# Splitting the first loads of a fused add and LayerNorm into 8-row transfers

## The chip, the cores and the metric

One core of a Trainium2 chip. The metric is device microseconds of the whole program on that core. A change of 2% would be 4.8 us.

## The reference

```python
z = x + residual                       # x, residual: (16, 1024, 512) float32
mean = np.mean(z, axis=-1, keepdims=True)
var = np.var(z, axis=-1, keepdims=True)
z_norm = (z - mean) / np.sqrt(var + eps)
return (gamma * z_norm + beta).astype(np.float32)
```

The 16,384 vectors of 512 numbers are laid over 128 partitions, so each partition has 128 of them. The kernel calls one such step of all partitions a "row": 128 x 512 x 4 bytes, 262,144 bytes. There are 128 rows of x, 128 of the residual and 128 of the output to move: 384 row moves.

## The kernel before

All transfers are issued from the sync engine's queue, in the order of a plan. `x48+16` is a load of rows 48 to 63 of x, `r` is the residual, `o` an output store.

```python
PLAN = """
x0+8 r0+8 x8+8 r8+8 x16+16 r16+16 x32+16 r32+16 x48+16
o0+16 r48+16 x64+12 o16+20 r64+16 x76+24 r80+16 o36+28
r96+16 x100+8 x108+20 r112+4 r116+12
o64+16 o80+28 o108+12 o120+4 o124+4
"""
```

Buffers hold 64 rows of x (reused for the result) and 32 rows of the residual (reused for the sum). Three kinds of issue therefore wait, and as the sync engine issues in order, everything behind a waiting issue waits too:

```python
if kind == "x":                                  # its z rows must have been stored
    while gone < len(stores) and stores[gone][0] < lo + n - Z_ROWS:
        nc.sync.wait_ge(so[gone], 16)            # the store has landed
        gone += 1
    ...
elif kind == "r":                                # its r rows must have been used
    if lo + n > R_ROWS:
        last = (lo + n - R_ROWS) // TURN - 1
        nc.sync.wait_ge(s_rstd[last % Z_TURNS], last // Z_TURNS + 1)
    ...
else:                                            # the result must be there
    nc.sync.wait_ge(s_out, lo + n)
```

The compute goes in turns of 4 rows: POOL adds, ACT makes the mean and the sum of squares with two passes per row and then the root, DVE normalises with two passes per row.

```python
nc.gpsimd.tensor_tensor(out=z, in0=part(zbuf, Z_ROWS, lo, n), in1=z, op=ALU.add)   # z: the r rows
...
act.activation(out=junk_m[k][:, :], in_=part(rbuf, R_ROWS, r, 1), func=ACT.Identity,
               scale=-inv_d, accum_out=column(nm, r))
...
act.activation(out=junk_s[k][:, :], in_=part(rbuf, R_ROWS, r, 1), func=ACT.Square,
               bias=column(nm, r), accum_out=column(ssq, r))
...
dve.scalar_tensor_tensor(out=part(zbuf, Z_ROWS, r, 1), in0=part(rbuf, R_ROWS, r, 1),
               scalar=column(nm, r), in1=gamma_p[:, :], op0=ALU.add, op1=ALU.mult)
# then reciprocal -> s_rstd (frees the r rows), then the second pass -> s_out
```

## Time and profile before

| | before |
|---|---|
| time, median of 3 runs | 237.92 us (237.81 to 237.95) |
| span of the profiled run | 236.5 us |
| bytes moved | 67.11 MB read, 33.55 MB written |
| busy: DVE, ACT, POOL | 75%, 78%, 61% |
| transfers on the sync queue | 27 |

The span is from the first to the last instruction; the time is about 1.4 us longer. The prediction below shows the slices, the queue, the chain and the waits. The groups of instructions give the durations that it works with: count, busy time, mean of one in ns, then the engine's idle time ahead of the group and what ended most of it.

```profile
L178 POOL TENSOR_TENSOR rbuf<-zbuf,rbuf 128x2048 f32<-128x2048 f32 x32 | 143.9, 4526 | 66.6 <-DMA rbuf<-in_residual_dram 62.1
L201 ACT ACTIVATE junk_m<-rbuf 128x512 f32<-128x512 f32 x128 | 74.3, 580 | 32.7 <-POOL rbuf L178 32.5
```

The large idle times on the right are what invites the change: POOL waits 62 us for loads, ACT 32 us for POOL. One of ACT's waits is the hole that the prediction speaks of, before its fifth turn:

```profile
45.98 0.60 ACT L201 ACTIVATE junk_m<-rbuf 128x512 f32<-128x512 f32 x1 [6.15 <-POOL rbuf L178]
```

### The profile page before, as it was taken

To read this page: it belongs to the slowest core of one execution; us is meant where nothing else is said; L and a number is where in the kernel's file an instruction comes from. 1 tells how busy PE (TensorE), PEld (TensorE's weight loads), DVE (VectorE), ACT (ScalarE), POOL (GpSimd) and SP (SyncE) were. 2 spreads that over 40 slices of the span, in tenths; PEclk is the share of its full clock that TensorE was granted. 3 is DMA by queue.
4 is the path that set the end of the run, shared out by engine and by line. 5 is a ranking of instruction groups with operands and counts; after the bars stand their busy time and mean duration, and the time that the engine had idled before them with its cause. 6 is when DMAs were issued, how large, how long until landed. Compare 5 with 4: busy or idle time off the path is not lost.

```text
span 236.5 us, 992 instructions
## 1 busy us (share of the span) xinstructions
PE 3.7 (2%) x4; PEld 1.2 (0%) x4; DVE 177.2 (75%) x290; ACT 183.8 (78%) x545; POOL 144.1 (61%) x36
## 2 busy tenths in 40 slices
PE   0600000000000000000000000000000000000000
PEld 0100000000000000000000000000000000000000
DVE  0001999629999999589990999889993999999930
ACT  2019997299999996899909999899939999999400
POOL 0098920999799306993079846993199498960000
DMA  8999999999999999998999999989999999998997
GB/s 316 438 435 435 421 438 443 443 443 443 427 371 438 443 421 423 470 436 384 443 449 474 391 427 499 398 389 432 416 454 429 417 442 435 489 436 388 411 410 327
DMA packets 3893, 100.68 MB, mean 426 GB/s; under 512 B 434, under 2 KB 434, under 8 KB 436
## 3 DMA queue, kind: packets, MB, share of 16 engines
q1 hardware_dynamic: 3888, 100.67, 99.4%
q14 instruction: 1, 0.01, 0.0%
q10 hardware_dynamic: 4, 0.00, 0.0%
HBM read 67.11 MB, written 33.55 MB: 426 GB/s over the span
## 4 chain that ended last, share of the span: by engine, by line
ACT 48%; DMA 35%; POOL 6%; DVE 4%; issue 1%; SPq 1%; ACTq 0%; DVEq 0%; POOLq 0%
DMA rbuf<-in_residual_dram 35%; ACT junk_s L211 25%; ACT junk_m L201 21%; POOL rbuf L178 6%; DVE zbuf L239 3%; ACT std L220 2%; DVE zbuf L253 1%; SPq L140 1%; DVE rstd L247 0%; ACTq L194 0%; DVEq L231 0%; ACTq L199 0%; POOLq L175 0%; ACTq L195 0%
## 5 line engine op out<-in xcount | busy, mean ns | idle before, releaser
L178 POOL TENSOR_TENSOR rbuf<-zbuf,rbuf 128x2048 f32<-128x2048 f32 x32 | 143.9, 4526 | 66.6 <-DMA rbuf<-in_residual_dram 62.1
L239 DVE SCALAR_TENSOR_TENSOR zbuf<-rbuf,nm,gamma_p 128x512 f32<-128x512 f32 x128 | 87.1, 743 | 46.5 <-ACT std L220 46.5
L201 ACT ACTIVATE junk_m<-rbuf 128x512 f32<-128x512 f32 x128 | 74.3, 580 | 32.7 <-POOL rbuf L178 32.5
L211 ACT ACTIVATE junk_s<-rbuf,nm 128x512 f32<-128x512 f32 x128 | 88.8, 694 | 1.0
L253 DVE SCALAR_TENSOR_TENSOR zbuf<-zbuf,rstd,beta_p 128x512 f32<-128x512 f32 x128 | 87.1, 743 | 1.1
L201 ACT ACTIVATION_READ_ACCUMULATOR junk_m<-rbuf 128x1 f32 x128 | 23.9, 187 | 0.0
L211 ACT ACTIVATION_READ_ACCUMULATOR junk_s<-rbuf,nm 128x1 f32 x128 | 23.9, 187 | 0.0
L220 ACT ACTIVATE std<-ssq,eps_t 128x4 f32<-128x4 f32 x32 | 9.5, 297 | 1.0
L247 DVE RECIPROCAL rstd<-std 128x4 f32<-128x4 f32 x32 | 5.4, 170 | 0.0
L192 ACT ACT_TABLE_LOAD x1 | 1.3, 1283 | 2.7 <-PEq L60 2.7
L131 PE MATMUL gamma_p<-gb_row,ones 1*128 1x512 f32 x2 | 2.0, 1118 | 7.0 <-DMA gb_row<-in_gamma_dram 7.0
L131 PE MATMUL beta_p<-gb_row,ones 1*128 1x512 f32 x2 | 1.9, 1052 | 0.0
L126 DVE MEMSET ones<- 1x128 f32 x1 | 0.2, 165 | 2.0 <-PEq L60 2.0
L131 PEld LDWEIGHTS beta_p<-gb_row,ones 1*128 1x128 f32 x2 | 0.7, 327 | 1.0 <-issue 0.5
L131 PEld LDWEIGHTS gamma_p<-gb_row,ones 1*128 1x128 f32 x2 | 0.5, 308 | 7.0 <-issue 7.0
L294 POOL MEMSET const-float32-0.0<- 128x1 f32 x1 | 0.1, 100 | 0.2 <-issue 0.2
L294 POOL MEMSET const-bfloat16-1.0<- 128x1 bf16 x1 | 0.1, 103 | 0.0
L294 POOL MEMSET const-uint8-127<- 128x1 uint8 x1 | 0.1, 103 | 0.0
L294 POOL MEMSET const-float32-1.0<- 128x1 f32 x1 | 0.1, 100 | 0.0
L127 DVE MEMSET eps_t<- 128x1 f32 x1 | 0.1, 59 | 0.0
## 6 DMA issues: line engine op xcount, KB each, us to landing
rbuf<-in_residual_dram SPq DMA_DIRECT2D x6, 4096.0 KB, 21.5
out_dram<-zbuf SPq DMA_DIRECT2D x2, 7168.0 KB, 31.5
zbuf<-in_x_dram SPq DMA_DIRECT2D x3, 4096.0 KB, 28.8
out_dram<-zbuf SPq DMA_DIRECT2D x2, 4096.0 KB, 33.9
zbuf<-in_x_dram SPq DMA_DIRECT2D x3, 2048.0 KB, 14.5
zbuf<-in_x_dram SPq DMA_DIRECT2D x1, 6144.0 KB, 24.0
out_dram<-zbuf SPq DMA_DIRECT2D x1, 5120.0 KB, 28.9
zbuf<-in_x_dram SPq DMA_DIRECT2D x1, 5120.0 KB, 26.3
```

What stands on the lines that cost most here:

```text
L126: nc.vector.memset(ones[:, :], 1.0).then_inc(s_const, 1)
L131: nc.tensor.matmul(dest[:, :], ones[:, :], gb_row[:, k * D : (k + 1) * D], start=True, stop=True).then_inc(s_pe, 1)
L140: i = nc.sync.dma_start(out=out, in_=in_).then_inc(s, 16)
L178: nc.gpsimd.tensor_tensor(out=z, in0=part(zbuf, Z_ROWS, lo, n), in1=z, op=ALU.add).then_inc(s_sum[lo // TURN % R_TURNS], 1)
L192: act.preload_act_table_set("sqrt_and_others")
L201: i = act.activation(out=junk_m[k][:, :], in_=part(rbuf, R_ROWS, r, 1), func=ACT.Identity, scale=-inv_d, accum_out=column(nm, r),)
L211: i = act.activation(out=junk_s[k][:, :], in_=part(rbuf, R_ROWS, r, 1), func=ACT.Square, bias=column(nm, r), accum_out=column(ssq, r),)
L220: act.activation(out=column(std, rows[0], TURN), in_=column(ssq, rows[0], TURN), func=ACT.Sqrt, bias=eps_t[:, 0:1], scale=inv_d,).then_inc ...
L239: dve.scalar_tensor_tensor(out=part(zbuf, Z_ROWS, r, 1), in0=part(rbuf, R_ROWS, r, 1), scalar=column(nm, r), in1=gamma_p[:, :], op0=ALU.ad ...
L247: dve.reciprocal(out=column(rstd, rows[0], TURN), in_=column(std, rows[0], TURN)).then_inc(s_rstd[j], 1)
L253: i = dve.scalar_tensor_tensor(out=z, in0=z, scalar=column(rstd, r), in1=beta_p[:, :], op0=ALU.mult, op1=ALU.add,)
L294: nc = _bacc.Bacc("TRN2", target_bir_lowering=False, num_devices=1)
```

## The change

The intent is to give the compute its first rows in smaller pieces, so that it starts and frees its buffers sooner. Only the plan changes. All loads up to row 63 have 8 rows; the second round's x loads are grouped anew.

```diff
 PLAN = """
-x0+8 r0+8 x8+8 r8+8 x16+16 r16+16 x32+16 r32+16 x48+16
-o0+16 r48+16 x64+12 o16+20 r64+16 x76+24 r80+16 o36+28
-r96+16 x100+8 x108+20 r112+4 r116+12
-o64+16 o80+28 o108+12 o120+4 o124+4
+x0+8 r0+8 x8+8 r8+8 x16+8 r16+8 x24+8 r24+8 x32+8 r32+8 x40+8 r40+8
+x48+8 r48+8 o0+16 x56+8 r56+8 x64+16 o16+20 r64+16 x80+20 r80+16 o36+28
+r96+16 x100+8 x108+20 r112+4 r116+12 o64+16 o80+28 o108+12 o120+4 o124+4
 """
```

## The prediction

> **What bounds the kernel now.** I read the page first: the busy shares, the 40 slices, the queues and the chain. No compute engine is above 78%, but the DMA row has no gap and its queue is charged with 99.4% of the sixteen engines' time.
>
> ```profile
> span 236.5 us, 992 instructions
> PE 3.7 (2%) x4; PEld 1.2 (0%) x4; DVE 177.2 (75%) x290; ACT 183.8 (78%) x545; POOL 144.1 (61%) x36
> DMA  8999999999999999998999999989999999998997
> GB/s 316 438 435 435 421 438 443 443 443 443 427 371 438 443 421 423 470 436 384 443 449 474 391 427 499 398 389 432 416 454 429 417 442 435 489 436 388 411 410 327
> ...
> q1 hardware_dynamic: 3888, 100.67, 99.4%
> ...
> HBM read 67.11 MB, written 33.55 MB: 426 GB/s over the span
> ```
>
> Only the first slice (start-up) and the last (completion) move clearly less than the mean. A low slice such as 371 or 384 is followed by a high one, so that is mostly how bytes fall into slices.
>
> The chain of work that ended last says something else at first sight: 48% ACT and 35% residual loads.
>
> ```profile
> ACT 48%; DMA 35%; POOL 6%; DVE 4%; issue 1%; SPq 1%; ACTq 0%; DVEq 0%; POOLq 0%
> ```
>
> It must not be read as the bound. It goes back from the last DVE instruction, which ends at 226.87 us, while the span ends at 236.5: the last 9.6 us are stores. The list of waits shows that the waits of POOL on loads and of ACT on POOL are the compute side starving behind a full queue:
>
> ```profile
> POOL rbuf L178 <- DMA rbuf<-in_residual_dram: 62.1, 9, 11.9
> DVE zbuf L239 <- ACT std L220: 46.5, 32, 20.5
> ACT junk_m L201 <- POOL rbuf L178: 32.5, 6, 12.8
> ```
>
> Last, the sync queue's timeline (when each transfer is issued) and the time to landing of single issues, by narrow windows of the DMA view. The first line below is r8+8, the second the last store, o124+4.
>
> ```profile
> 2.29 0.43 SPq L140 DMA_DIRECT2D rbuf<-in_residual_dram  x1
> 3.78 0.48 SPq L140 DMA_DIRECT2D zbuf<-in_x_dram  x1
> 42.70 0.33 SPq L140 DMA_DIRECT2D rbuf<-in_residual_dram  x1
> 150.34 0.33 SPq L140 DMA_DIRECT2D rbuf<-in_residual_dram  x1
> ```
> ```profile
> rbuf<-in_residual_dram SPq DMA_DIRECT2D x1, 2048.0 KB, 19.6
> zbuf<-in_x_dram SPq DMA_DIRECT2D x1, 4096.0 KB, 47.2
> out_dram<-zbuf SPq DMA_DIRECT2D x1, 1024.0 KB, 9.6
> ```
>
> The store of 1 MB takes 9.6 us although 1 MB at 426 GB/s is 2.5 us: even the very last transfer stands behind others. So r8+8 landed at 2.29 + 19.6 = 21.9 us and x32+16 at 3.78 + 47.2 = 51.0 us. The kernel is one full FIFO of 384 row moves (128 rows of x, of r and of out, 262,144 bytes each) with a start-up ahead and a completion behind it.
>
> **What the Trainium skill says.** "DMA: Bandwidth & Descriptors", section "Queues, rings and completion order": each DMA engine consumes descriptors in ring order. The trace agrees: the early loads land in the order of issue, at 7.2, 12.1, 17.0, 21.9 us. The same page, "Anatomy of one DMA": a fixed part of about 2.0 us per DMA plus bytes / 436 GB/s (fitted there for another issuing path). The first 2 MB transfer, issued at 0.00, landed after 7.2 us; the fit gives 2.0 + 4.8 = 6.8. The next ones came 4.9 us apart, with no 2 us between them, so a fixed part is hidden wherever the queue is full. "Perfetto Trace Analysis", section "DMA Optimizations": splitting may finish sooner "if DMA engines are generally idle"; here they are not, so that reason for splitting is absent.
>
> **The change part by part.** Six loads of 16 rows (x16, r16, x32, r32, x48, r48) become twelve of 8; x64+12 and x76+24 become x64+16 and x80+20 (same rows, same count); the tail from r96 on is the same. 27 transfers on this queue become 33; bytes, arithmetic and stores are unchanged.
>
> (1) Cost per split. Two 8-row loads, x8 and r8, took from 12.1 (r0's landing: 0.43 + 11.7) to 21.9: 9.8 us for 16 rows. Three 16-row loads took from 21.9 to 51.0: 29.1 us, 9.7 each. A split therefore costs about 0.1 us, and six cost 0.6 us. This lies on the path, because the queue is the path. It is a small difference of rounded numbers; I allow 0 to 0.2 us each.
>
> (2) Does the queue ever run dry? I write the new order down with 2.3 us of start-up (7.2 - 4.9), 4.9 us per 8-row transfer and 0.607 us per row (9.7/16) for the rest, and ask for each gated issue whether it comes 2.3 us before the queue would be empty. Compute durations are those of the chain: POOL 4.53 us per 4 rows; ACT 2.46 + 2.94 + 0.30 and two gaps of 0.02, 5.74 per 4 rows; DVE 2.82 to the reciprocal that frees r slots.
> Nine loads are free at once: work until 2.3 + 9 x 4.9 = 46.4. r32+8 now waits only for rows 0 to 7, whose reciprocal ended at 31.2. r40+8 waits for rows to 15, as r32+16 did: 42.7, queue until 56. Then r16+8 has landed by about 32 instead of 41.3, so ACT goes on without the hole of 6.15 us before its fifth turn: rows 23 free at 42.7 + 2 x 5.74 = 54.2 (r48+8; queue until 66), rows 31 at 65.7 (r56+8; queue until 85). x64+16 waits for store o0+16 to land, about 81; x56 and r56 still stand behind it, 9.8 us. x80+20 waits for o16+20, about 112; r64+16 stands behind it, 9.7 us. r80+16 needs rows to 63, about 112. r96+16 needs rows to 79: r64 lands at 122, + 4.5 POOL + 23.0 ACT + 2.8 DVE = 152.5, while o36+28 fills the queue until 160.9. x100+8 waits for that store with r96+16 (9.7 us) behind it. r116+12 needs rows to 95: about 175, queue until 190. The thinnest is r96+16 with 8.4 - 2.3 = 6 us to spare. No bubble.
>
> (3) The tail. Before, POOL started the last three adds at 197.5 and DVE ended 29.4 us later; o124 was issued at 226.9 and its turn in the FIFO came near 234. If all of it moves by 0.6 us, the same 4 to 5 us of cushion remain after the start-up of a transfer.
>
> (4) The gain. ACT loses its hole near 40 us and is up to 6 us ahead in the first half. This removes idle time of engines off the bound: worth 0. By r96 the compute is tied to the landing of r64 and r80 again.
>
> Sum: 237.92 + 0.6 = 238.5 us; span about 237.1.
>
> **The rivals.** *Early start wins.* ACT is 78% busy and on the chain; if it were the bound, the 6.15 us hole would come off: about 232. For it speaks the chain alone; against it the unbroken DMA row and the queue still standing in front of o124. A saving would need a faster queue. *Each transfer pays its fixed part.* Six times 2.0 us would give 250. The spacing of 4.9 us in a full queue against 4.8 us of bare bytes speaks against it. *Smaller pieces run slower.* In the slices 8-row loads show 435 GB/s and 16-row loads 443; taken literally, 25.2 MB would take 57.9 instead of 56.8 us: +1.1 us, 239.0. The landings say half of that. *A new bubble.* r96+16 or one of the three loads behind a store could come late; every microsecond beyond 6 would show fully. *Other reads beside writes.* Stores move in the order; slices with both vary from 371 to 499 GB/s, and x48+16 seems about 0.8 us late by its slices, so half a microsecond may appear or vanish either way.
>
> **Range and chances.** Three runs of before lie within 0.14 us. From 0 to 0.2 us per split and half a microsecond of mixing I get 237.6 to 239.5. A 2% change is 4.8 us: faster needs a moved bound (0.01), slower a bubble or a paid fixed cost (0.02); within 2%, 0.97.
>
> **What would show it.** In the changed profile the DMA row should stay at 9 without a new low slice, the queue at 99% with 33 transfers; 8-row loads should land 4.9 us apart to r48; the reciprocal should release r32+8 near 31 us and ACT should have no hole at 40; r96+16 should be issued near 153 and o124 near 227.5, landing some 9.6 us later; POOL's waits on loads should be more in number but not less in total by much. I am wrong if a slice shows the queue empty, if o124 lands 4 us after issue (the tail bound by compute), or if the spacing of 8-row loads is not 4.9 us.

(A slip of its text: "The first line below is r8+8, the second the last store" fits neither of the two fences after it. The four issues are r8+8, x32+16, r32+16 and r96+16; the three landings are r8+8, x32+16 and o124+4.)

## The result

| | before | changed |
|---|---|---|
| time, median of 6 runs | 237.94 us | 238.19 us |
| range | 237.72 to 238.22 | 238.0 to 238.31 |
| ratio, 95% interval | | 1.0009 (0.9996 to 1.0022) |
| span of the profiled run | 236.5 us | 236.7 us |
| transfers on the sync queue | 27 | 33 |

A ratio here is the mean time of one kernel's runs over the mean of the other's of the same rounds, so it is not quite the ratio of the two medians. The kernel is the same within 2%; the difference, some 0.2 us, is not clear of the noise.

First the page of the changed kernel: span, busy engines, the DMA row and rate in 40 slices, the queue.

```profile
span 236.7 us, 1002 instructions
PE 3.7 (2%) x4; PEld 1.2 (0%) x4; DVE 177.2 (75%) x290; ACT 183.5 (78%) x545; POOL 144.3 (61%) x36
DMA  8999999999999999999999999979999999999897
GB/s 316 438 429 429 429 440 418 426 440 418 426 440 443 402 440 476 388 443 421 443 426 429 474 443 465 456 325 438 421 435 436 442 415 432 500 446 397 384 424 321
...
q1 hardware_dynamic: 4752, 100.67, 99.4%
```

The queue is as full as before (99.4%). The one digit 7 belongs to 325 GB/s between slices of 456 and 438; it is bytes shifted to the slices around it, not an empty queue: the store o36+28, which runs there, took 17.23 us by the mean of its landings, against 17.19 before.

Now the waits (who waited for whom: us in total, times, longest; the lines of this kernel have numbers one lower, as its plan is a line shorter):

```profile
POOL rbuf L177 <- DMA rbuf<-in_residual_dram: 63.0, 12, 22.5
...
ACT junk_m L200 <- POOL rbuf L177: 32.8, 3, 17.4
```

The change did what it intended and got nothing for it. ACT no longer has its hole of 6.15 us before the fifth turn, but its idle time in total is the same, 32.8 us against 32.5: six waits have become three, and the longest is now 17.4 us, just before rows 64 to 67. The compute ran ahead in the first half and then stood waiting for the queue.

The sync queue's timeline shows the gates (start us, duration). The lines chosen are the issues of r32+8, r40+8, r48+8, r56+8, then x64+16, r96+16:

```profile
31.24 0.33 SPq L139 DMA_DIRECT2D rbuf<-in_residual_dram  x1
...
42.73 0.33 SPq L139 DMA_DIRECT2D rbuf<-in_residual_dram  x1
...
54.22 0.33 SPq L139 DMA_DIRECT2D rbuf<-in_residual_dram  x1
...
65.71 0.33 SPq L139 DMA_DIRECT2D rbuf<-in_residual_dram  x1
80.89 0.33 SPq L139 DMA_DIRECT2D zbuf<-in_x_dram  x1
...
152.44 0.33 SPq L139 DMA_DIRECT2D rbuf<-in_residual_dram  x1
```

And the last store, o124+4: its issue, and its time to landing in the DMA view of a narrow window.

```profile
226.87 0.33 SPq L139 DMA_DIRECT2D out_dram<-zbuf  x1
```
```profile
out_dram<-zbuf SPq DMA_DIRECT2D x1, 1024.0 KB, 9.8
```

It is issued at 226.87 us, as before, and still stands some 7 us behind other stores. The end of the kernel is the end of the queue.

Where did six splits go? The trace records when each of the sixteen DMA engines finishes its share of a transfer. After 96 row moves (four splits) the changed kernel's landings are 0.33 us later than before, both for the last engine and for the mean: 0.08 us a split. After 112 row moves they are 0.36 us *earlier* in the last engine (0.08 in the mean). The gain is not the changed kernel's: its r48+8 took 4.89 us, as every 8-row load. It is a loss of the kernel before, whose x48+16 took 10.47 us in the last engine (10.21 in the mean) instead of the 9.71 of each 16-row load ahead of it. At the end the difference is +0.13 us (last engine; mean +0.05). So two terms of about half a microsecond nearly cancel: six splits, and a stall that the kernel before has and the changed one has not. This is read from one trace of each kernel; the times can't show it, as the experiments tell.

### The profile page after: what moved, and what is told of

It is laid out like the page before. It is cut to its first block, busy times and chain, and to the rows that moved or that the text cites. A ratio compares the mean times of both kernels' runs of the same rounds, so it can differ in the third digit from the quotient of the medians.

```text
span 236.7 us, 1002 instructions
## 1 busy us (share of the span) xinstructions
PE 3.7 (2%) x4; PEld 1.2 (0%) x4; DVE 177.2 (75%) x290; ACT 183.5 (78%) x545; POOL 144.3 (61%) x36
## 3 DMA queue, kind: packets, MB, share of 16 engines
q1 hardware_dynamic: 4752, 100.67, 99.4%
## 4 chain that ended last, share of the span: by engine, by line
ACT 58%; DMA 26%; POOL 6%; DVE 4%; issue 1%; SPq 0%; ACTq 0%; DVEq 0%; POOLq 0%
ACT junk_s L210 30%; DMA rbuf<-in_residual_dram 26%; ACT junk_m L200 25%; POOL rbuf L177 6%; DVE zbuf L238 3%; ACT std L219 3%; DVE zbuf L252 1%; SPq L139 0%; DVE rstd L246 0%; ACTq L193 0%; DVEq L230 0%; ACTq L198 0%; POOLq L174 0%; ACTq L194 0%
## 5 line engine op out<-in xcount | busy, mean ns | idle before, releaser
L200 ACT ACTIVATE junk_m<-rbuf 128x512 f32<-128x512 f32 x128 | 74.2, 580 | 33.0 <-POOL rbuf L177 32.8
## 6 DMA issues: line engine op xcount, KB each, us to landing
out_dram<-zbuf SPq DMA_DIRECT2D x1, 5120.0 KB, 31.2
```

The costliest lines, as they stand in the source:

```text
L200: i = act.activation(out=junk_m[k][:, :], in_=part(rbuf, R_ROWS, r, 1), func=ACT.Identity, scale=-inv_d, accum_out=column(nm, r),)
```

## The experiments

Theories. *Queue*: the time is start-up, one full queue of 384 row moves, and completion; every extra load transfer costs about 0.08 us; compute and its waits are hidden as long as a gated issue comes before the queue is empty. *Early start*: what the compute gets sooner or later decides. *Fixed cost*: each transfer pays the 2 us that the prediction quotes. A second question is the stall at x48+16. The figures are medians; "before" is the kernel before on the same chip.

| run | time | before there | ratio (95%) |
|---|---|---|---|
| splits only | 238.24 | 237.77 | 1.0018 (1.0001 to 1.0035) |
| all loads 4 rows | 241.63 | 237.77 | 1.0160 (1.0143 to 1.0177) |
| thin compute, plan of before | 237.60 | 237.77 | 0.9993 (0.9977 to 1.0010) |
| thin compute, changed plan | 237.96 | 237.77 | 1.0008 (0.9991 to 1.0024) |
| store moved back | 241.41 | 238.10 | 1.0138 (1.0122 to 1.0153) |
| compute started late | 238.24 | 238.10 | 1.0006 (0.9990 to 1.0021) |
| only x48 split | 238.01 | 238.10 | 0.9995 (0.9982 to 1.0009) |
| before again | 237.90 | 238.10 | 0.9995 (0.9981 to 1.0009) |
| pieces of 4 rows | 241.87 | 237.90 | 1.0162 (1.0145 to 1.0180) |
| changed, x48+16 | 238.19 | 237.90 | 1.0008 (0.9991 to 1.0024) |
| regrouped only | 237.85 | 237.90 | 0.9994 (0.9977 to 1.0010) |
| merged loads | 245.70 | 237.90 | 1.0330 (1.0312 to 1.0347) |

### Splits alone, and the regrouping alone

```diff
-x16+16 r16+16 x32+16 r32+16 x48+16
+x16+8 x24+8 r16+8 r24+8 x32+8 x40+8 r32+8 r40+8 x48+8 x56+8
-o0+16 r48+16
+o0+16 r48+8 r56+8
```

> Only the splitting: six 16-row loads become twelve 8-row loads in place, with the order, the 12/24-row x loads and the tail of before; 33 transfers. Queue theory (the DMA queue is never empty and each extra transfer costs about 0.08 us): +0.5 us over before, 238.4. Early-start theory (compute gets its rows earlier and that is what the change buys or loses): r16 still lands at about 42 us here, so this kernel should equal before, 237.9, and the order alone would make the difference of the changed kernel. Fixed-cost theory (2 us per transfer uncovered): +12 us, 250.

Measured 238.24 against 237.77, ratio 1.0018; the interval (1.0001 to 1.0035) takes in the changed kernel's 1.0009. The last of r16's rows land as late as before (41.5 us), but the first eight at 36.6, so ACT's hole near 40 us is smaller, not kept:

```profile
41.26 0.60 ACT L201 ACTIVATE junk_m<-rbuf 128x512 f32<-128x512 f32 x1 [1.44 <-POOL rbuf L178]
```

This kernel thus separates the order from the splits less cleanly than expected; still, the earlier rows of the changed plan are worth nothing that shows. The landing records repeat the changed kernel's in the mean of the engines: +0.34 us after 96 row moves, -0.07 after 112 (no stall), +0.05 at the end. Its slowest engine ends 0.36 us later, and that engine sets the time. The other half alone:

```diff
-x64+12 ... x76+24
+x64+16 ... x80+20
```

> Only the other part of the change: x64+12 and x76+24 of before become x64+16 and x80+20, 27 transfers. Queue theory: no cost, 237.9 within 0.3; the gates it moves (x64 on o0, x80 on o16) keep 7 us of cover.

Measured 237.85 against 237.90: nothing that shows, as expected.

### The compute taken away

Every pass over the rows works on 8 columns, in both plans: 8 of a row's 512 on ACT and DVE, 8 of a turn's 2,048 in POOL's adds. The root and the reciprocal, and all waits and transfers, stay. The result is wrong.

```diff
-            out=z, in0=part(zbuf, Z_ROWS, lo, n), in1=z, op=ALU.add
+            out=z[:, 0:8], in0=part(zbuf, Z_ROWS, lo, n)[:, 0:8], in1=z[:, 0:8], op=ALU.add
```

(and so for both ACT passes and both DVE passes)

> Wrong result on purpose: the plan of before with every compute instruction on 8 of 512 columns, so that the engines are nearly idle and all waits and transfers stay. Queue theory: the DMA alone is the time, so within 0.3 us of before, 237.6 to 238.2. Early-start or compute theory: several us faster than before.

> Wrong result on purpose: the plan of the changed kernel with every compute instruction on 8 of 512 columns. Queue theory: 0.3 to 0.6 us over the same with the plan of before, 238.2 to 238.5, as no wait for compute is left that could hide or add anything. If the measured difference of only 0.25 us came from a compute gain that paid part of the splits, the difference here should be the full 0.5 us; if it came from chance in the queue, it varies.

The page of the first of them, busy engines and DMA row:

```profile
PE 3.7 (2%) x4; PEld 1.2 (0%) x4; DVE 42.8 (18%) x290; ACT 76.5 (32%) x545; POOL 5.8 (2%) x36
...
DMA  8999999999999999999999899899999999998998
```

POOL fell from 144 to 6 us, ACT from 184 to 77, DVE from 177 to 43, and the time from 237.77 to 237.60. This is the plainest result: the 78% busy ACT, 48% of the chain before, is worth 0.17 us in the medians, and by the interval of the ratio not over 0.55. The difference of the two thin kernels is 237.96 - 237.60 = 0.36 us, between the 0.25 and the 0.5 that the expectation set against each other; with intervals of 0.4 us to either side the times can't choose. The landing records have the same two terms as with the compute in place: +0.29 us in the mean after 96 row moves, +0.07 after 112, +0.18 at the end. Nothing there points to a hidden compute gain.

### The compute started later

```diff
-x0+8 r0+8 x8+8 r8+8
+x0+8 x8+8 r0+8 r8+8
```

> The changed kernel with x0 x8 r0 r8 instead of x0 r0 x8 r8: the first add can start only at about 17 us instead of 12, and all compute of the first half comes about 5 us later. Queue theory: every gated issue is still on time (the thinnest, r48+8, with about 4.7 us to spare), so the same as the changed kernel, 238.2 within 0.3. Early-start theory: up to 5 us slower, 243.

Measured 238.24 against 238.10, ratio 1.0006, while the changed kernel had 1.0009. The first rows are complete one 8-row transfer later (POOL's first add starts at 17.26 us instead of 12.25) and it costs nothing that shows.

### The cost of a split: dose, and pieces against transfers

Every load of the changed plan in 4 rows, 72 transfers:

> Dose: every load of the changed kernel cut to 4 rows, 64 loads and 8 stores, 72 transfers, 45 more than before. Queue theory: 45 x 0.08 = 3.6 us over before, 241.5 (between 241 and 242.5), no empty queue. Early-start theory: rows land for compute earlier still, so no slower than the changed kernel, 238. Fixed-cost theory: tens of us.

Measured 241.63, +3.86 us for 45 transfers, 0.086 us each, where 0.08 was expected. Fixed costs of 2 us per transfer would have given +90 us. That the size fits so well is partly luck. In the mean of the engines the last landing is 2.95 us later: 45 splits of 0.077 us (below) less the stall of 0.5 us, which this kernel lacks. The rest comes from its slowest engine, which ends 1.56 us after the mean instead of 0.77.

The next kernel has the 27 transfers of before, but each partition's share comes in pieces of 4 rows (8 KB), because the rows are dealt out of DRAM in blocks of 4 (`move` cuts both sides of a transfer alike):

```diff
-        b0 = lo - lo % BLOCK
-        v = t[P * b0 : P * (b0 + BLOCK), :].rearrange("(p j) d -> p j d", p=P)
-        return v[:, lo - b0 : lo - b0 + n, :].rearrange("p a b -> p (a b)")
+        return t[P * lo : P * (lo + n), :].rearrange("(c p j) d -> p c (j d)", p=P, j=4)
```

> The 27 transfers of before, same order and bytes, but the rows are dealt out of DRAM in blocks of 4, so that each partition's share of a transfer comes in pieces of 8 KB instead of one piece of 8 to 56 KB: 768 data pieces per DMA engine instead of 216, no transfer more. If the cost of a split belongs to the pieces (the kernel with all loads of 4 rows pays some 3.7 us for 360 more pieces, 10 ns each): 552 x 10 ns = 5.5 us, 243.4 (242 to 244.5). If it belongs to the transfers (their issue and completion): 237.9.

The queue's lines (packets, MB, share) show the pieces: 3,888 packets before, then this kernel, then the one with all loads of 4 rows.

```profile
q1 hardware_dynamic: 12720, 100.67, 100.1%
```
```profile
q1 hardware_dynamic: 10368, 100.67, 99.6%
```

Measured 241.87, +3.97 us for 552 more pieces per engine and not one transfer more. The landing records of loads in a full queue (mean of the engines) settle where the cost of a split lies:

| 16 rows of loads as | pieces per engine | us |
|---|---|---|
| one transfer (before) | 8 | 9.71 |
| two transfers (changed) | 16 | 9.79 |
| four transfers (all loads 4 rows) | 32 | 9.94 |
| one transfer in pieces of 4 rows (this kernel) | 32 | 9.94 |

With 32 pieces it makes no difference whether they are one transfer or four. A split costs 0.077 us, its eight extra pieces at 9.5 ns each; nothing of it is left for the transfer as such. The layout in DRAM changes with this edit too; the two equal figures speak against an effect of it.

The whole kernel pays less, 7.2 ns a piece (3.97 us / 552), where 10 ns were expected (5.5 us, 242 to 244.5). It lacks the stall (0.5 us), and pieces of stores cost less: the 88 more of them behind the last load take 0.36 us, 4 ns each.

### What an empty queue costs

One store of the changed plan moved, so that x64+16 waits for it with nothing left in the queue:

```diff
-x48+8 r48+8 o0+16 x56+8 r56+8 x64+16 o16+20
+x48+8 r48+8 x56+8 r56+8 o0+16 x64+16 o16+20
```

> The changed kernel with one store moved: o0+16 behind x56+8 and r56+8 instead of ahead of them, so that x64+16, which waits for that store to land, has nothing ahead of it in the queue any more. Queue theory: the queue runs empty once,[...] and all of it shows at the end: 238.2 + 2.6 = 240.8, with one slice of low DMA share near 91 us. If waits of the sync queue are harmless as such: 238.2. It also places the first store near 81 us: a stall of the loads near 68 us that follows the clock stays at 68, one that follows the first store moves to about 79.

The windows of this kernel from 84 to 96 us (the last two columns are the DMA share and the rate) and the landing of x64+16, issued at 90.45:

```profile
84.00:88.00 4.00, 0.00 (x0) 0.00 (x0) 3.82 (x7) 3.97 (x14) 4.00 (x2) 1.00 0.91 393
88.00:92.00 4.00, 0.00 (x0) 0.00 (x0) 3.79 (x8) 3.93 (x13) 1.92 (x1) 1.00 0.77 262
92.00:96.00 4.00, 0.00 (x0) 0.00 (x0) 3.96 (x7) 3.97 (x13) 0.00 (x0) 1.00 0.83 360
```
```profile
zbuf<-in_x_dram SPq DMA_DIRECT2D x1, 4096.0 KB, 13.3
```

The rate falls to 262 GB/s just there. Measured 241.41; by the ratios (1.0138 against 1.0009 of 238) that is 3.1 us above the changed kernel instead of the expected 2.6 (an estimate whose working isn't on record). In the profiled run, the slowest of the four (241.93), the span is 3.9 us longer (240.6 against 236.7). The start-up of 2.3 us (7.2 - 4.9, from the first transfer) is there: 2.3 + 9.7 = 12.0 of the 13.3 us. Another 1.3 us went in x64's own last pieces, ahead of store o16+20, where the pieces ran slow as in the stall told below. By the landing records 3.8 us of delay are still there at the end, which is what the queue theory says of a bubble.

### Merging too far

```diff
-x32+16 r32+16 x48+16 o0+16 r48+16 x64+12 o16+20 r64+16 x76+24
+x32+32 r32+16 o0+16 r48+16 x64+16 o16+20 r64+16 x80+20
-x100+8 x108+20 ... o120+4 o124+4
+x100+28 ... o120+8
```

> The other direction: before with loads merged, x32+32, x64+16, x80+20, x100+28 and o120+8, 23 transfers. Splits alone would give -0.3 us. But x100+28 lands only at about 187 us, so rows 100 on are added 12 us later, the last rows end after the queue has run dry, and the tail becomes bound by compute: the gates worked out by the durations of the trace give an end near 245 us of span, 246.6 of time, with empty slices near the end. If the queue alone counted and large transfers were always better: 237.6.

Measured 245.70, close to the 246.6 worked out from durations. The timeline of POOL, and the window from 236 to 240 us:

```profile
187.50 31.39 POOL L177 TENSOR_TENSOR rbuf<-zbuf,rbuf 128x2048 f32<-128x2048 f32 x7 [12.43 <-DMA zbuf<-in_x_dram]
```
```profile
236.00:240.00 4.00, 0.00 (x0) 0.00 (x0) 1.95 (x3) 0.00 (x0) 0.00 (x0) 1.00 0.31 131
```

POOL waits 12.43 us for the 28-row load and then has seven adds to make in a row; the last rows come after the queue has run dry. It is the only kernel that compute bounds at its end. Transfer size matters here, by 8 us, where it sets the last rows, and by tenths where it does not.

### The stall ahead of the first store

> The kernel before once more (its plan broken into other lines, same text otherwise), for the noise of the comparison and for a second trace. Ratio 1.000 within 0.001. If the stall in x48+16 belongs to this order of transfers, the trace has it again at the same place (10.2 to 10.5 us for x48+16); if it was chance, x48+16 takes 9.7 us.

Two kernels with the same text give a ratio of 0.9995: differences of 0.1 us can't be told apart by time. But the trace repeats. In the second trace, as in the trace of before, r32+16 and x48+16 take 18.0 and 28.1 us from issue to landing (DMA view):

```profile
rbuf<-in_residual_dram SPq DMA_DIRECT2D x1, 4096.0 KB, 18.0
...
zbuf<-in_x_dram SPq DMA_DIRECT2D x1, 4096.0 KB, 28.1
```

Issued at 42.65 and 43.02, they land at 60.7 and 71.1: 10.5 us apart instead of 9.7. The landing records give 10.45 here, 10.47 in before, 10.46 with the regrouping alone and 10.18 with thin compute, so it is neither chance nor compute. In the kernel with the store moved back, the pieces that run longer than usual (up to 1.05 us instead of 0.61) start not near 68 us but from 77 to 79, just ahead of its first store, whose pieces start at 79: slow pieces go with the first store, not with the clock. The changed kernel has a few of them too, up to 0.81 us, but its landings are not late.

> Before with only x48+16 cut into x48+8 and x56+8: 28 transfers. In the trace of before x48+16 took 10.5 us instead of 9.7, a stall of the mean landing of about 0.57 us that the kernels with 8-row loads there do not have. If cutting the load ahead of the first store avoids that stall: faster than before by 0.57 - 0.08 = 0.5 us, about 237.4. If the stall has another cause or 16-row loads as such are not to blame: 0.08 slower, 238.0.

Measured 238.01 against 238.10, a ratio of 0.9995 where 0.5 us, 0.998, was expected: a miss. (The 0.57 us that it starts from is 0.50 in the landing records, 10.21 less 9.71.) In its trace x56+8 takes 5.13 instead of 4.89 us, so the stall was only halved, and the time can't show what is left.

> The changed kernel with one load back to 16 rows, x48+16, as the last load ahead of the first store o0+16 (32 transfers). If a 16-row load ahead of the first store brings the stall of before back: x48+16 takes 10.2 to 10.5 us in the trace and the time is about 238.2 - 0.1 + 0.5 = 238.6. If the size of that load does not matter: x48+16 takes 9.7 us and the time is 238.1.

Measured 238.19 against 237.90. Its r40+8 was issued at 42.92 and its x48+16 at 43.29 us; the DMA view has their landings:

```profile
zbuf<-in_x_dram SPq DMA_DIRECT2D x1, 4096.0 KB, 27.7
rbuf<-in_residual_dram SPq DMA_DIRECT2D x1, 2048.0 KB, 18.3
```

They land at 71.0 and 61.2 us: no stall (9.72 us in the landing records). So a 16-row load right ahead of the first store is not enough to bring it, and the simple explanation falls. What fits all traces is weaker: the kernels whose loads from x16 to r32 have 16 rows or more show the stall (10.2 to 10.5 us for 16 rows; a quarter of a microsecond where only x48 is split), and those whose loads there come in pieces of 4 or 8 rows show 0.1 us or none. Why is left open, and so is the slow end of x64+16 in the kernel with the store moved back, ahead of its second store.

## Why the prediction was right

**The bound.** The queue stayed full and set the end; thin compute settles it (237.60 against 237.77). Reading the chain of waits as the bound would have given about 232, as the prediction says of this rival.

**Cost per split.** Predicted 0.1 us from rounded landings, with 0 to 0.2 allowed; measured 0.08 in the landings of the changed trace. Six make 0.5 us, not 0.6.

**No bubble.** The gates worked out by hand came as said: 31.2, 42.7, 54.2, 65.7, 81, 112 (112.45), 152.5 (152.44; its own terms, 122 + 4.5 + 23.0 + 2.8, add up to 152.3). In another experiment, moving one store across two loads turned one of these gates into a bubble of some 3 us, so the check of the gates was needed.

**The tail.** It was said to move by 0.6 us; it did not move, as r116+12, which it waits for, landed at 197.37 us against 197.40: POOL starts its last adds at 197.44 and o124 is issued at 226.87, both as before.

**The gain of zero.** ACT's hole did vanish and its total idle time did not change, as said; the late start confirms it.

**Too high by 0.35 us.** The prediction added 0.6 us (238.5) and the changed kernel added 0.25 (238.19). The splits cost 0.5, and the sum lacks the stall of before at x48+16. The text noticed it ("seems about 0.8 us late") but put it under mixing that may go either way. In the traces it belongs to this order of loads: 0.50 us in the mean of the engines (0.76 in the last), of which 0.37 to 0.45 us last to the end, and the changed kernel is without it. Against +0.5 us of splits it left +0.13 us in the last engine and +0.05 in the mean. So the measured difference is near zero because two terms happen to cancel. That is read from traces; the experiment that should have shown the stall in time (only x48 split) missed, and the noise of the times is as large as either term. The range, 237.6 to 239.5, held; its own terms give 237.4 to 239.6.

**Against the rivals.** Fixed cost per transfer is out by a factor of 25 (0.08 against 2 us). Slower small pieces are right, and they are the whole cost of a split: 9.5 ns a piece, with half the size that the slices suggested (0.5 us for six splits, not 1.1).

## What to carry to other kernels

When the DMA row has no gap and the last store still queues, engines that wait for loads are a result of the bound and not the bound: giving them data earlier moves their idle time and nothing else. Then cost an issue plan by two things: some ns for each piece (here 9.5 for loads, 4 for stores, in pieces of 8 KB and more), and for each gated issue whether it comes a start-up (here 2.3 us) before the queue runs empty; the second can cost microseconds, the first took tenths here, and 4 us where all loads were cut to 4 rows. A kernel with nearly all its arithmetic taken away, and all its waits left in, tells in one run how much any change of the compute could bring (here 0.2 us, within 0.55; no plan tried here beat the kernel before beyond the noise).

## What the Trainium skill lacked or had wrong

- "DMA: Bandwidth & Descriptors", section "Anatomy of one DMA", gives about 2.0 us per DMA, fitted for another issuing path, and doesn't say what one more transfer costs in a full queue. Here it was about 0.08 us; only the first transfer (7.2 us for 2 MB) and the bubble (2.3 us of start-up) showed the 2 us.
- The same page, section "Why small descriptors are slow (HBM only)", works its overhead per packet out for 256 bytes and gives no figure for large pieces. Pieces of 8 KB instead of 8 to 56 KB still cost 3.97 us for 552 more per engine: 9.5 ns each in loads, 4 ns in stores.
- The same page, section "Where 436 GB/s comes from", says that for transfers between HBM and SBUF the HBM side, about 358 GB/s, binds. Taken alone that does not hold here: this case moved 426 GB/s over the whole span. The 425 GB/s of 16 MB that the same section quotes as measured agrees with it. (What the neighbouring core did is not recorded.)
- No page tells of the loss ahead of the first store in a queue: 0.74 to 0.76 us in the last engine in the traces of before, 0.47 with thin compute, and 0.1 or none where the loads from x16 to r32 come in pieces of 4 or 8 rows.
- No page says how much the queue takes in before the issue itself blocks. With 81 entries per engine issued at the start (the changed kernel) each issue took 0.3 to 0.5 us; with all loads of 4 rows the twelfth issue took 1.5 us and the next four 2.1 us each, at roughly a hundred entries. It cost nothing that shows: the queue stayed full.
